# The last gathered tile of an expert mixer: second product on VectorE instead of TensorE

## The chip, the cores and the metric

One core of a Trainium2 chip runs the whole kernel in one launch. The metric is the device time of one execution in microseconds (us). The median of three executions before the change is 4364.15 us (4361.64 to 4384.96).

## What is computed

The reference is one layer of an encoder over 1280 tokens (a prompt of 256 and a sample of 1024) of width 1024, in fp32. After two mixing branches and a residual sum `x`, each token passes through a mixer of experts. It picks 16 of 16384 experts in each of 8 heads, 128 in all, and with `z` the normed token it computes

```python
u = jnp.take(u_tab, eidx, axis=0)
ve = jnp.take(v_tab, eidx, axis=0)
act = jax.nn.gelu(jnp.einsum('td,thkd->thk', zt, u).astype(jnp.float32), approximate=False) * g
return jnp.einsum('thk,thkd->td', act.astype(zt.dtype), ve)
```

`g` is a softmax over the scores of the picks. The result is added to `x`, and a last norm gives the output. The first einsum is called the u product here, the second one the second product, or v product. Both tables have 16384 rows of 1024 floats (64 MB each).

## The kernel before

The 1280 tokens are ten tiles of 128. Four tiles of the sample are *dense*: they multiply with both whole tables on TensorE (`dense`). The other six are *gathered*: for each token only the 128 picked rows of each table are fetched, by indirect DMAs that POOL issues. One such DMA fetches one row of 4 KB for each of the 128 partitions, 512 KB in all.

`experts(routes)` (L1095) walks over gathered tiles. In one turn it interleaves `u_steps` of one tile with `v_steps` of the tile before it, and a last turn runs the v product of the last tile by itself. Two of the gathered tiles belong to the prompt and go through a call of their own (L1172). The other four (`r0 + r1`, two in each list) go through the call in L1217, and `dense` is written right behind it in L1220.

- `u_steps` (L928): a slot is one of the 128 picks. Tokens lie on the partitions: POOL gathers row `ei[:, s]` of `peer_u` into a buffer `ug` (L938), and VectorE multiplies it with the normed tokens `zs` and sums along the row, in one scalar_tensor_tensor (L940).
- `v_steps` (L951): here the 128 picks of one token lie on the partitions (`eit` is the transposed index), so a gather (L969) fetches what one token needs, and TensorE sums over the partitions: the token's column of the transposed weights `actT`, put on a diagonal of a zeroed tile `zt` (L962, L963), is the stationary operand of 128 rows by 32 columns. Four gathers make a group. When the fourth is there, 16 matmuls follow (L976; two halves of 512 columns, each with four matmuls of 32 columns in four column groups of the array, and the trace has two records for each such fp32 matmul). So one tile has 32 groups and 512 records. All sums stay in one PSUM tile `acc`. At the end the residual row block is loaded by a POOL DMA (L982), added (L983), and `finish` (L992) norms the rows and stores them.
- `ring` (L925): every gathered row block, of u and of v, takes one of seven buffers of 512 KB, in the order in which the program asks for them. A buffer of v is free only when the matmuls of its group have read it.
- `dense` (L1048): one block is 128 experts; there are 128 blocks. `first(b)` loads a 512 KB block of the transposed u table, splits it into a high and a low part (L123 on ACT, L124 on VectorE), multiplies it in 24 matmuls of 512 columns (L140 to L142), applies Gelu (L1065), the weights (L1067) and another split (L159, L160). `second(g)` does this for four blocks of the v table, in 96 matmuls for each half of the columns, and adds the results into a tile in SBUF on VectorE (L1081). That is 48 matmuls a block. The loads of both tables go through the SP queue, 1 MB a block, into two raw buffers each.

The order of the instructions on each engine is fixed when the program is built (`tile.TileContext(nc, schedule_with_timeline_sim=True)`, L1293): a planner with simulated times takes, for an engine that is free, the ready instruction of the highest priority, where what is written earlier goes first. `experts` raises the steps of the v product above that:

```python
if vs:
    with tc.high_priority():
        if next(vs, "end") == "end":
            vs = None
```

At run time an engine executes its instructions in that order, and an instruction that waits holds up all that stands behind it on its engine.

Of the kernel before, what the change touches and what calls it, by code (L numbers as in the profile page):

```python
# [12 lines left out]
F32 = mybir.dt.float32  # L13
# [6 lines left out]
OP = mybir.AluOpType  # L20
# [4 lines left out]
P = 128  # L25
D = 1024
# [19 lines left out]
def ap_of(base, dims):  # L46
    return bass.AP(tensor=base.tensor, offset=base.offset, ap=[list(base.ap[0])] + [list(d) for d in dims])
# [3 lines left out]
def encoder(ctx, tc, I, O, dbg=None):  # L51
    nc = tc.nc
# [52 lines left out]
    x2d = dram.tile([T, D], F32, name="x2d")  # L105
# [67 lines left out]
    def rsqrt_small(pool, out, src, inv_n, shape, name):  # L173

        v = pool.tile(shape, F32, name=name + "v", tag=name + "v", bufs=2)
        t = pool.tile(shape, F32, name=name + "t", tag=name + "t", bufs=2)
        nc.vector.tensor_scalar(out=v, in0=src, scalar1=inv_n, scalar2=EPS, op0=OP.mult, op1=OP.add)  # L177
        nc.vector.tensor_single_scalar(out=t.bitcast(I32), in_=v.bitcast(I32), scalar=1, op=OP.logical_shift_right)  # L178
        nc.vector.tensor_scalar(out=out.bitcast(I32), in0=t.bitcast(I32), scalar1=-1.0, scalar2=float(0x5F3759DF),  # L179
                                op0=OP.mult, op1=OP.add)  # L180
        for _ in range(3):
            nc.vector.tensor_tensor(t, out, out, op=OP.mult)  # L182
            nc.vector.scalar_tensor_tensor(out=t, in0=t, scalar=-0.5, in1=v, op0=OP.mult, op1=OP.mult)  # L183
            nc.vector.scalar_tensor_tensor(out=out, in0=t, scalar=1.5, in1=out, op0=OP.add, op1=OP.mult)  # L184
# [740 lines left out]
    def ring(name):  # L925
        return pe_.tile([P, D], F32, name=name, tag="ring", bufs=RING)

    def u_steps(route):  # L928
        tt, gw, ei = route["tt"], route["gw"], route["ei"]
        zs = pe_.tile([P, D], F32, name="zs", tag="zs")  # L930
        nc.gpsimd.dma_start(zs, x2d[tt:tt + P])
        gffn = ring("gffn")
        nc.sync.dma_start(gffn, I["norm_ffn"].partition_broadcast(P))
        nc.vector.scalar_tensor_tensor(out=zs, in0=zs, scalar=route["rt"], in1=gffn, op0=OP.mult, op1=OP.mult)
        dots = pe_.tile([P, P], F32, name="dots", tag="dots", bufs=2)
        for s in range(P):
            ug = ring("ug")
            nc.gpsimd.indirect_dma_start(out=ug, out_offset=None, in_=I["peer_u"],  # L938
                                         in_offset=bass.IndirectOffsetOnAxis(ap=ei[:, s:s + 1], axis=0))
            nc.vector.scalar_tensor_tensor(out=ug, in0=ug, scalar=1.0, in1=zs, op0=OP.mult, op1=OP.mult,  # L940
                                           accum_out=dots[:, s:s + 1])
            yield
        act = pe_.tile([P, P], F32, name="act", tag="act", bufs=2)
        nc.scalar.activation(out=act, in_=dots, func=AF.Gelu)
        nc.vector.tensor_tensor(act, act, gw.rearrange("p h k -> p (h k)"), op=OP.mult)
        route["act"] = act
        yield
# [3 lines left out]
    def v_steps(route):  # L951
        tt, eit = route["tt"], route["eit"]
        acc = pps.tile([P, D], F32, name="acc", tag="acc")
        nc.tensor.transpose(acc[:, 0:P], route["act"], ident)  # L954
        actT = pe_.tile([P, 4, 32], F32, name="actT", tag="actT", bufs=2)
        nc.vector.tensor_copy(actT.rearrange("p g i -> p (g i)"), acc[:, 0:P])
        zt = zts[0]
        for b in range(8):

            h = b % 2  # L960
            o = (b + 6) % 8 * 4
            nc.vector.memset(ap_of(zt[:, h, 0, 0, o:o + 1], [[128, 4], [33, 4]]), 0.0)  # L962
            nc.vector.tensor_copy(ap_of(zt[:, h, 0, 0, b * 4:b * 4 + 1], [[128, 4], [33, 4]]), actT[:, :, b * 4:b * 4 + 4])  # L963
            for i in range(4):
                vgs = []
                for g in range(4):
                    t = g * 32 + b * 4 + i
                    vg = ring("vg")
                    nc.gpsimd.indirect_dma_start(out=vg, out_offset=None, in_=I["peer_v"],  # L969
                                                 in_offset=bass.IndirectOffsetOnAxis(ap=eit[:, t:t + 1], axis=0))  # L970
                    vgs.append(vg)
                    if g == 3:

                        for n in range(2):
                            for g_, v_ in reversed(list(enumerate(vgs))):
                                nc.tensor.matmul(acc[g_ * 32:(g_ + 1) * 32, n * 512:(n + 1) * 512], zt[:, h, g_, i],  # L976
                                                 v_[:, n * 512:(n + 1) * 512], start=b == 0 and i == 0,
                                                 stop=b == 7 and i == 3, tile_position=(0, g_ * 32), skip_group_check=True)
                    yield
        y = ring("y")  # L980
        x2r = ring("x2r")
        nc.gpsimd.dma_start(x2r, x2d[tt:tt + P])  # L982
        nc.vector.tensor_tensor(y, acc, x2r, op=OP.add)  # L983
        finish(y, x2r, tt)
        yield

    def final_gain():
        gfin = ring("gfin")
        nc.sync.dma_start(gfin, I["norm_final"].partition_broadcast(P))
        return gfin  # L990

    def finish(y, sq, tt, gfin=None):  # L992
        gfin = final_gain() if gfin is None else gfin
        ss = pe_.tile([P, 1], F32, name="fss", tag="fss")
        nc.scalar.activation(out=sq, in_=y, func=AF.Square, accum_out=ss)
        rs = pe_.tile([P, 1], F32, name="frs", tag="frs")
        rsqrt_small(pe_, rs, ss, 1.0 / D, [P, 1], "fin")
        nc.vector.scalar_tensor_tensor(out=y, in0=y, scalar=rs[:, 0:1], in1=gfin, op0=OP.mult, op1=OP.mult)  # L998
        nc.gpsimd.dma_start(O["y"][tt:tt + P], y)  # L999
# [48 lines left out]
    def dense(routes, zt, acc, dp, up, bankS, bankV):  # L1048
# [37 lines left out]
        for g in range(P // GE):  # L1086
            for b in range(g * GE + 1, (g + 1) * GE + 1):
                if b < P:
                    first(b)
            second(g)  # L1090
        gfin = final_gain()
        for t, r in enumerate(routes):
            finish(acc[:, t], ring("sq"), r["tt"], gfin)

    def experts(routes):  # L1095
        prev = None
        for r in routes + [None]:
            us = u_steps(r) if r else iter(())
            vs = v_steps(prev) if prev else iter(())
            while us or vs:  # L1100
                if us and next(us, "end") == "end":
                    us = None
# [4 lines that stand above are left out]
            prev = r  # L1107
# [13 lines left out]
    with ExitStack() as pctx:  # L1121
# [23 lines left out]
        ap = fctx.enter_context(tc.tile_pool(name="A1", bufs=1, side="left"))  # L1145
# [23 lines left out]
    for h in range(NH):  # L1169
        hgrn_out(s0, SS, h, 0, hp, 2, bankH)  # L1170
    next(prs)
    experts(rP)  # L1172
    fctx.close()
    vs_ = vsp.tile([P, 8, 512], F32, name="vs", tag="vs")
# [39 lines left out]
    up0 = ctx.enter_context(tc.tile_pool(name="DU0", bufs=1, side="right"))  # L1214
    tctx.close()
    rd, r1 = rs[:ND // P], rs[ND // P:]
    experts(r0 + r1)  # L1217
    acc = ctx.enter_context(tc.tile_pool(name="DA", bufs=1, side="left")).tile([P, ND // P, D], F32, name="acc")
    up = ctx.enter_context(tc.tile_pool(name="DU", bufs=1, side="left"))
# [78 lines left out]
```

## Time and profile before

| | before |
|---|---|
| median of 3 executions | 4364.15 us |
| the profiled execution | 4369.98 us |
| its span | 4368.2 us |
| PE busy | 3901.4 us (89%) |
| DVE busy | 2947.0 us (67%) |
| ACT busy | 1560.6 us (36%) |
| POOL busy | 1725.3 us (39%) |
| DMA | 1264.02 MB, mean 289 GB/s |

All readings below are from the profiled execution. PE is TensorE, DVE is VectorE, ACT is ScalarE, POOL is GpSimd and SP is the engine that issues most of the plain loads. The shares are means over stages that have different limits, so they say little by themselves; the slices and the tables by windows show one stage at a time. Times in them count from the start of the span. A line in a row is a line of the kernel; a helper's line stands for all of its callers.

### The profile page before, as it was taken

What the parts mean: (1) busy time and instruction counts of PE and PEld (TensorE: products, weight loads), DVE (VectorE), ACT (ScalarE), POOL (GpSimd) and SP (SyncE); (2) the same over time, 40 slices, a digit from 0 to 9 for tenths busy, and PEclk for the clock granted to TensorE, in tenths of its full rate; (3) what the DMA queues carried; (4) which work ended last, traced back from release to release, by engine and by line L of the source; (5) the groups of instructions that cost most, each with busy time, mean ns of one, the idle gap of its engine ahead of it and who ended that gap; (6) DMA issues with size and microseconds to landing.
All of it is one profiled execution on the core that took longest, in us unless ns stands there. A gap on an engine that the chain in (4) does not pass through costs nothing. (4 is left out here: it accounts for less than half of the span.)

```text
span 4368.2 us, 56612 instructions
## 1 busy us (share of the span) xinstructions
PE 3901.4 (89%) x19232; PEld 2747.1 (63%) x19232; DVE 2947.0 (67%) x7782; ACT 1560.6 (36%) x2600; POOL 1725.3 (39%) x1565
## 2 busy tenths in 40 slices
PE   7998999997687979868987399999999999999998
PEld 5787777774435733346543165777777777776676
DVE  4637987568987765876679875566666666643344
ACT  5555455453233224422101387322222222222222
POOL 0000743344444344765445312445444545434400
PEclk9999999998889999889999699999999999999999
DMA  5464999889989988999878668999999999888842
GB/s 161 124 188 136 362 342 332 314 316 319 326 288 325 330 306 286 316 345 337 311 280 283 229 234 318 331 325 339 332 335 322 344 325 346 322 317 311 309 142 67
DMA packets 508322, 1264.02 MB, mean 289 GB/s; under 512 B 49920, under 2 KB 203136, under 8 KB 505984
## 3 DMA queue, kind: packets, MB, share of 16 engines
q0 software_dynamic: 224352, 816.94, 52.0%
q1 hardware_dynamic: 197056, 354.05, 23.9%
q10 hardware_dynamic: 86624, 89.40, 5.9%
q8 instruction: 152, 2.49, 0.2%
q14 instruction: 138, 1.13, 0.1%
HBM read 1165.05 MB, written 95.16 MB: 288 GB/s over the span
## 5 line engine op out<-in xcount | busy, mean ns | idle before, releaser
L969 POOL DMA_INDIRECT vg<-peer_v,eit x768 | 823.9, 1073 | 1072.1 <-PE acc L976 429.5
L938 POOL DMA_INDIRECT ug<-peer_u,ei x768 | 887.2, 1155 | 868.7 <-DVE ug L940 407.5
L940 DVE SCALAR_TENSOR_TENSOR ug<-ug,zs 128x1024 f32<-128x1024 f32 x768 | 932.2, 1220 | 380.9 <-DMA ug<-peer_u,ei 318.7
L976 PE MATMUL acc<-vg,zt 128*32 128x512 f32 x3072 | 402.1, 644 | 126.1 <-DMA vg<-peer_v,eit 125.7
L140 PE MATMUL pm<-zth,uh 128*128 128x512 f32 x1024 | 406.7, 397 | 1.1 <-ACT gs L1039 1.1
L141 PE MATMUL pm<-ztl,uh 128*128 128x512 f32 x1024 | 405.9, 396 | 0.0
L142 PE MATMUL pm<-zth,ul 128*128 128x512 f32 x1024 | 405.7, 396 | 0.0
L140 PE MATMUL pm<-vh,ah 128*128 128x512 f32 x1024 | 399.7, 393 | 1.6 <-DVE acc L1081 1.6
L141 PE MATMUL pm<-vl,ah 128*128 128x512 f32 x1024 | 401.0, 392 | 0.0
L142 PE MATMUL pm<-vh,al 128*128 128x512 f32 x1024 | 399.3, 392 | 0.0
L123 ACT CAST vh<-vraw 128x512 fp32r<-128x512 f32 x256 | 158.3, 620 | 662.1 <-DMA vraw<-peer_v 368.0
L138 PE MATMUL pm<-xg,wraw 128*128 128x256 f32 (+1 forms) x1024 | 297.3, 443 | 4.3 <-DVE sr L855 4.3
L976 PEld LDWEIGHTS acc<-vg,zt 128*32 128x32 f32 x3072 | 83.8, 114 | 329.1 <-issue 171.8
L140 PE MATMUL pm<-hh,wh 128*128 128x512 f32 x672 | 268.7, 400 | 2.8 <-ACT gt L240 0.9
L141 PE MATMUL pm<-hl,wh 128*128 128x512 f32 x672 | 267.2, 398 | 0.0
L142 PE MATMUL pm<-hh,wl 128*128 128x512 f32 x672 | 265.3, 395 | 0.0
L1081 DVE TENSOR_TENSOR acc<-pm,acc 128x512 f32<-128x512 f32 x256 | 173.9, 688 | 126.7 <-PE pm L142 113.5
L124 DVE TENSOR_TENSOR vl<-vraw,vh 128x512 fp32r<-128x512 f32 x256 | 173.6, 689 | 119.7 <-ACT vh L123 96.2
L124 DVE TENSOR_TENSOR ul<-uraw,uh 128x1024 fp32r<-128x1024 f32 x128 | 156.6, 1223 | 140.7 <-ACT uh L123 129.6
L138 PEld LDWEIGHTS pm<-xg,wraw 128*128 128x128 f32 x1024 | 193.6, 195 | 83.0 <-issue 58.4
L140 PEld LDWEIGHTS pm<-zth,uh 128*128 128x128 f32 x1024 | 192.2, 188 | 61.4 <-issue 11.7
L140 PEld LDWEIGHTS pm<-vh,ah 128*128 128x128 f32 x1024 | 192.2, 188 | 60.0 <-issue 11.7
(361 smaller groups left out, 7263.6 us busy)
## 6 DMA issues: line engine op xcount, KB each, us to landing
uraw<-uT SPq DMA_DIRECT2D x128, 512.0 KB
vraw<-peer_v SPq DMA_DIRECT2D x256, 256.0 KB
wraw<-wi SPq DMA_DIRECT2D x84, 512.0 KB
gd<-gs ACTq DMA_DIRECT2D x16, 2048.0 KB
g<-gd ACTq DMA_DIRECT2D x32, 1024.0 KB
wraw<-wq SPq DMA_DIRECT2D x48, 512.0 KB
wraw<-wo SPq DMA_DIRECT2D x24, 512.0 KB
ug<-peer_u,ei POOLq DMA_INDIRECT x768
```

What stands on the lines that cost most here:

```text
L123: nc.scalar.copy(hi, src)
L124: (eng or nc.vector).tensor_tensor(lo, src, hi.bitcast(F32), op=OP.subtract)
L138: nc.tensor.matmul(out, w[0], x[0], start=start, stop=stop)
L140: nc.tensor.matmul(out, w[0], x[0], start=start, stop=False)
L141: nc.tensor.matmul(out, w[0], x[1], start=False, stop=False)
L142: nc.tensor.matmul(out, w[1], x[0], start=False, stop=stop)
L938: nc.gpsimd.indirect_dma_start(out=ug, out_offset=None, in_=I["peer_u"], in_offset=bass.IndirectOffsetOnAxis(ap=ei[:, s:s + 1], axis=0))
L940: nc.vector.scalar_tensor_tensor(out=ug, in0=ug, scalar=1.0, in1=zs, op0=OP.mult, op1=OP.mult, accum_out=dots[:, s:s + 1])
L969: nc.gpsimd.indirect_dma_start(out=vg, out_offset=None, in_=I["peer_v"], in_offset=bass.IndirectOffsetOnAxis(ap=eit[:, t:t + 1], axis=0))
L976: nc.tensor.matmul(acc[g_ * 32:(g_ + 1) * 32, n * 512:(n + 1) * 512], zt[:, h, g_, i], v_[:, n * 512:(n + 1) * 512], start=b == 0 and i == ...
L1081: nc.vector.tensor_tensor(acc[:, t, ns], pm, acc[:, t, ns], op=OP.add)
```

## The change

A new generator `v_slots` does the second product with tokens on the partitions, as the u product does: it loads the residual rows into an SBUF tile `vacc`, gathers the picked rows of `peer_v` slot by slot with the index `ei`, and adds each, times the token's weight, with one scalar_tensor_tensor on VectorE. It needs neither transposed weights nor PSUM. A route that has an `acc` takes it; only the last tile of `r1` gets one, and its pool takes 4 KB per partition of SBUF up to the end. The other five gathered tiles keep `v_steps`. The weights `act`, the ring of seven buffers and the priority of the v steps are as before.

```diff
+    def v_slots(route):
+
+        tt, ei, act = route["tt"], route["ei"], route["act"]
+        acc = route["acc"].tile([P, D], F32, name="vacc", tag="vacc", bufs=1)
+        nc.gpsimd.dma_start(acc, x2d[tt:tt + P])
+        for s in range(P):
+            vg = ring("vg")
+            nc.gpsimd.indirect_dma_start(out=vg, out_offset=None, in_=I["peer_v"],
+                                         in_offset=bass.IndirectOffsetOnAxis(ap=ei[:, s:s + 1], axis=0))
+            nc.vector.scalar_tensor_tensor(out=acc, in0=vg, scalar=act[:, s:s + 1], in1=acc, op0=OP.mult, op1=OP.add)
+            if s % 2:
+                yield
+        finish(acc, ring("sq"), tt)
+        yield
+
...
-            vs = v_steps(prev) if prev else iter(())
+            vs = (v_slots if "acc" in prev else v_steps)(prev) if prev else iter(())
...
+    vp = ctx.enter_context(tc.tile_pool(name="VA", bufs=1, side="right"))
+    for r in r1[1:]:
+        r["acc"] = vp
     experts(r0 + r1)
```

## Rows read from the trace of the kernel before

**Rows 1.** The page: the span, and PE, DVE, granted clock, DMA in 40 slices.
```profile
span 4368.2 us, 56612 instructions
...
PE   7998999997687979868987399999999999999998
...
DVE  4637987568987765876679875566666666643344
...
PEclk9999999998889999889999699999999999999999
DMA  5464999889989988999878668999999999888842
```
**Rows 2.** Windows of 100 us: length, PE, PEld, DVE, ACT, POOL busy, clock, DMA, GB/s.
```profile
3900.00:4000.00 100.00, 100.00 (x504) 67.92 (x505) 38.70 (x55) 26.12 (x38) 41.43 (x42) 1.00 0.89 312
4000.00:4100.00 100.00, 97.62 (x494) 65.85 (x493) 35.62 (x53) 24.22 (x36) 44.34 (x43) 1.00 0.88 310
...
4200.00:4300.00 100.00, 100.00 (x436) 81.48 (x435) 46.41 (x63) 29.44 (x43) 0.00 (x0) 1.00 0.36 110
```
**Rows 3.** Timeline of POOL around the start of the last tile's gathers: start, duration.
```profile
3826.91 0.94 POOL L969 DMA_INDIRECT vg<-peer_v,eit  x1 [0.30 <-issue]
3827.85 0.58 POOL L982 DMA_DIRECT2D x2r<-x2d  x1
3840.88 0.95 POOL L969 DMA_INDIRECT vg<-peer_v,eit  x1 [12.45 <-PE acc L976]
```
**Rows 4.** Waits from 3829 to 4160 us: total, times, longest.
```profile
POOL vg L969 <- PE acc L976: 151.4, 31, 12.4
...
PE acc L976 <- DMA vg<-peer_v,eit: 3.4, 3, 2.4
```
**Rows 5.** Timeline of PE: one group of the last tile between two dense matmuls.
```profile
4063.28 0.39 PE L142 MATMUL pm<-vh,al 128*128 128x512 f32 x1
...
4063.60 1.92 PE L976 MATMUL acc<-vg,zt 128*32 128x512 f32 x16
...
4065.45 0.50 PE L140 MATMUL pm<-vh,ah 128*128 128x512 f32 x1
```
**Rows 6.** The chain that ended last: the same step in two successive rounds of four blocks.
```profile
4279.52 0.47 PE pm L142 x2
4323.77 0.47 PE pm L142 x2
```
**Rows 7.** Groups on DVE from 4180 to 4312.75 us, twelve dense blocks alone.
```profile
L1081 DVE TENSOR_TENSOR acc<-pm,acc 128x512 f32<-128x512 f32 x24 | 16.6, 690 | 17.5 <-PE pm L142 17.4
L124 DVE TENSOR_TENSOR vl<-vraw,vh 128x512 fp32r<-128x512 f32 x24 | 16.5, 691 | 21.5 <-ACT vh L123 21.4
L124 DVE TENSOR_TENSOR ul<-uraw,uh 128x1024 fp32r<-128x1024 f32 x12 | 14.7, 1225 | 25.8 <-ACT uh L123 25.8
L160 DVE TENSOR_TENSOR al<-ge,ah 128x512 fp32r<-128x512 f32 x12 | 8.3, 691 | 6.2 <-ACT ah L159 6.2
L1067 DVE TENSOR_TENSOR ge<-ge,g 128x512 f32<-128x512 f32 x12 | 8.2, 685 | 0.0
```
**Rows 8.** Groups on DVE from 3829 to 4176 us.
```profile
L998 DVE SCALAR_TENSOR_TENSOR y<-y,frs,gfin 128x1024 f32<-128x1024 f32 x2 | 2.6, 1285 | 0.1
...
L983 DVE TENSOR_TENSOR y<-acc,x2r 128x1024 f32<-128x1024 f32 x2 | 2.4, 1214 | 2.3 <-PE acc L976 2.3
L963 DVE COPY zt<-actT 128x16 f32<-128x16 f32 x8 | 1.2, 168 | 10.4 <-issue 7.8 <-PE acc L976 2.6
```
**Rows 9.** Timeline where u gathers run alone, DVE and POOL.
```profile
1846.72 0.93 POOL L938 DMA_INDIRECT ug<-peer_u,ei  x1 [0.30 <-issue]
...
1850.34 1.22 DVE L940 SCALAR_TENSOR_TENSOR ug<-ug,zs 128x1024 f32<-128x1024 f32 x1
...
1851.49 1.22 DVE L940 SCALAR_TENSOR_TENSOR ug<-ug,zs 128x1024 f32<-128x1024 f32 x1
1851.53 1.99 POOL L938 DMA_INDIRECT ug<-peer_u,ei  x1 [0.30 <-issue]
```
**Rows 10.** Windows, columns as in rows 2, where u gathers run alone.
```profile
1800.00:1900.00 100.00, 76.32 (x355) 35.27 (x354) 94.26 (x183) 41.84 (x101) 78.05 (x63) 0.86 0.95 342
```
**Rows 11.** Windows of 50 us, columns as in rows 2: the highest DMA rate.
```profile
500.00:550.00 50.00, 47.24 (x212) 38.24 (x211) 49.56 (x114) 18.79 (x25) 34.78 (x26) 1.00 0.98 364
```
**Rows 12.** Waits from 1700 to 1900 us.
```profile
ACT pn L606 <- DVE mn L602: 54.5, 18, 6.6
PEld pm L138 <- ACT pn L606: 44.3, 17, 5.3
```
**Rows 13.** Windows: u and v gathers beside dense; all engines, then L938 alone on POOL.
```profile
3200.00:3300.00 100.00, 100.00 (x470) 74.61 (x469) 69.75 (x116) 28.85 (x44) 49.29 (x43) 1.00 0.93 332
...
3200.00:3300.00 100.00, 23.17 (x20) 1.00 0.93 332
```
**Rows 14.** The page: the costliest groups, the matmuls of the gathered v product.
```profile
L976 PE MATMUL acc<-vg,zt 128*32 128x512 f32 x3072 | 402.1, 644 | 126.1 <-DMA vg<-peer_v,eit 125.7
```

## The prediction

> **What bounds the kernel now.** I read the slices first, because the change touches one stage only. From slice 23 on, about 2500 us, PE shows nines to the end while DVE falls to 6 and then to 3 and 4 [rows 1]: the dense stage is bound by TensorE, and VectorE has room on average. Next the windows of 100 us. Around 4000 us PE is busy 98 to 100 us in 100, DVE 36 to 39, at full clock and with DMA at 0.88 [rows 2]. Third, POOL's timeline and the list of waits say what paces the gathers of the last tile. Its first one is issued at 3840.88, when a group of the tile before it frees its buffers [rows 3], and POOL waited 151 us in that stage for L976, while PE waited 3.4 us for gathers [rows 4]. So the ring sets the pace: a group of four must be complete and read before the next can be. POOL does nothing but that there: 42 or 43 gathers in 100 us, one in 2.35 us [rows 2].
>
> **What the change takes away.** One group lies between two dense matmuls that start 2.17 us apart [rows 5]. Four dense blocks, 192 matmuls, take 44.25 us [rows 6], so one takes 0.230 us and a block 11.06 us. The group costs 2.17 - 0.23 = 1.94 us, and the 32 groups of a tile **62 us** of an engine that has no other slack. The transpose and copy of the weights, 16 small writes of `zt` and the sum L983 go too, some 0.17 to 1.2 us each on DVE [rows 8]; with them under 5 us of DVE, counted at nothing since they wait for no one's path.
>
> **What it adds.** 128 scalar_tensor_tensors of 128x1024 on DVE. L940 has this form, with two fp32 operands in SBUF and a sum written out besides: back to back they start 1.15 us apart [rows 9]. L998, without that sum, shows 1.285 us [rows 8], pipeline ends included. I take 1.15 us, 147 us in all; with 1.285 it would be 164.
>
> The Trainium skill (Vector Engine (DVE) Microarchitecture Reference, Points that are easy to get wrong) says that this instruction with two non-bf16 sources in SBUF runs at half throughput; doubling the step measured back to back would make it 2.3 us, an estimate, and with the formulas below the sum +185 us instead of +61, 4549 us. The trace disagrees, with 1.15 us for that very form, and the measurement decides: that way gets no chance below.
>
> **What it moves.** The residual load, now the first DMA on POOL rather than the last, stands where L982 of the tile before is followed by 12.45 us of waiting [rows 3]: nothing, and without that cover 0.6 us. As many gathers as before are issued, but their buffers come free one by one, as with u. The end of the tile (norm and store) stays hidden behind dense work, which goes on for some 190 us after it now [rows 1, 2]. The 4 KB of SBUF show no price in the trace; I take none, since no tile of the stage is made smaller.
>
> **The wait it adds.** Each new DVE instruction waits for a gather, and behind it in DVE's fixed order stand the dense stage's splits, weights and sums. TensorE waits for those. One dense block needs (16.6 + 16.5 + 14.7 + 8.3 + 8.2) / 12 = 5.36 us of DVE [rows 7]. So the question is how much dense work the order puts between two slots. Call it w, in us of DVE. In the stage of the 128 slots DVE then does 128w / 5.36 = 23.9w blocks, which are 264w us of PE.
>
> The stage's length: if DVE sets it, 128 x (1.15 + w). If the DMA does, the bytes are 128 x 0.524 = 67.1 MB of gathers and 23.9w x 1.05 = 25.1w MB of tables. The nearest rows give 342 GB/s at 0.95 of the DMA's time [rows 10] and 364 at 0.98 [rows 11]; with the middle, 353, it is 190 + 71w us, which is the longer one up to w = 0.75. POOL gives about the same floor: where u gathers run alone, 63 are issued in 100 us [rows 10], 1.59 us each, and POOL is then busy 78 us with them and loses 0.3 us between two, 97 in all. An issue takes 0.93 us, and up to 1.99 while such DVE instructions run [rows 9].
>
> What PE can't do in that stage has to be done after it. The net change is the stage, minus 264w, minus the 62 us: **128 - 193w** while the DMA rules, 85 - 136w beyond.
>
> For w the trace of before has two ends. Where u gathers run alone, DVE is busy 94.26 us in 100, of which 63 x 1.15 = 72.5 are slots; that leaves 21.8 / 63 = 0.35 us [rows 10]. Where u and v gathers run together beside dense work, 20 u slots stand in 69.75 us of DVE, which leaves 2.3 us [rows 13]. The new stage is like the first: one kind of gather, with buffers freed one by one. In the second the groups of v held most of the ring. And the new slots have the raised priority, which u's have not, so the order takes a slot whenever it believes one to be ready, and dense work only in the gaps. The stage of u gathers alone also shows what follows [rows 10, 12]: PE at 76 us in 100, with 54.5 us of ACT waiting for a small DVE result and 44.3 us of PE's weight loads waiting for that ACT. With w = 0.35 the stage is 215 us, in which PE does 92 us of dense work; it loses 123 and gets 62 back. The sum is **+61 us**. On the profiled execution, 4370 us, that is 4431; it lies 5.8 us above the median of the runs, from which I forecast 4364 + 61 = **4425 us**. If w goes to 0, which [rows 10] can't exclude, it is +128 us.
>
> PE's clock in such a stage: with PE at 76 us in 100 the mean granted was 0.86, between the levels of 1.2 and 2.4 GHz [rows 10]. It costs nothing as long as DVE or the DMA, not PE, ends the wait, and full clock is there where PE is full [rows 2].
>
> **The rivals.** (1) *VectorE carries both; faster.* If the order leaves w = 1.08 or more, that is, if it expects a gather no oftener than every 2.23 us, PE never runs dry and the whole 62 us are gained: 4302 us. For it: the pace of 2.35 us and DVE at 36 to 39 us in 100 [rows 2], and the 2.3 us between slots beside dense work [rows 13]. Against: that pace was made by groups in the ring, which go, and where u gathers run alone one comes every 1.59 us [rows 10]. The point from which it is faster at all is w = 0.66. Chance 0.33, with a part of it between 4302 and 4342.
> (2) *It balances.* Around w = 0.66 the lost and gained time of PE cancel, 4342 to 4386 us. Nothing in the rows picks this value. Chance 0.09.
> (3) *Slots back to back.* If the order believes that gathers arrive as fast as POOL issues them undisturbed, 0.93 + 0.3 = 1.23 us [rows 9], w is 0.08 and the dense stage all but stops for 196 us: +113, 4477 us. There are pairs like that in the trace [rows 9], but no long run of them in the mean of 100 us [rows 10]. It is the upper part of my forecast, 0.15 of its 0.58.
> (4) *Not as stated.* If more or fewer than one tile took the new way, the count of L976 would not fall from 3072 [rows 14] to 2560. `r1` has two tiles and `r1[1:]` one, so I give this nothing.
>
> **How the numbers follow.** A measurement of this kernel can tell about 0.5% from no change, 22 us. Slower by more is the forecast, with (3): 0.58. Within it is (2): 0.09. Faster is (1): 0.33. Cases of both signs hold most of the chance, so the range takes in both: from 4298, the full gain with the few us of PE's waits for gathers, to 4480, w = 0.06. The slower case by itself is 4390 to 4480.
>
> **What the changed profile would show.** L976 x2560. A stretch after about 3840 us with 128 gathers in 200 to 230 us, DMA at 0.95 or more, DVE above 85 us in 100 with waits for `vg`, PE clearly below 80 us, and PE's loads or ACT waiting for DVE. After it dense work alone, 11.06 us a block, and an end that is later by the stage's lost time. I am wrong if PE stays full beside the slots: then w was over 1, and the gathers came no oftener than before. I am wrong in size if DVE idles for gathers that come slower than 1.7 us, or if an added slot takes clearly other than 1.15 us.

## The result and the profile after

The change is **faster**, by 1.4 to 1.9%: 4307.53 us median of four executions (4296.1 to 4308.96), against 4371.23 of the kernel before in the same runs. The measured ratio is 0.9833 with a 95% interval of 0.981 to 0.9856; the two medians alone give 0.985. I had forecast 4425 us and slower; 4302 us was the rival in which VectorE carries both. The profiled execution took 4296.1 us, with a span of 4294.2.

The slices of the changed kernel, PE and DVE:

```profile
span 4294.2 us, 55849 instructions
...
PE   6998999997777988878988389999999999999998
...
DVE  4637988567988774986679985566666666679974
```

PE has the same nines to the end as before [rows 1]. DVE now has 7 and 9 in the slices where it had 3 and 4. The windows of 100 us around 4000, columns as in rows 2:

```profile
3900.00:4000.00 100.00, 100.00 (x434) 81.19 (x433) 93.90 (x104) 30.26 (x47) 53.60 (x42) 1.00 0.96 338
4000.00:4100.00 100.00, 100.00 (x433) 80.98 (x432) 92.88 (x102) 27.36 (x42) 56.03 (x42) 1.00 0.95 336
```

DVE went from 36 to 39 us up to 93, DMA from 0.88 to 0.96 of the time, and PE is still full, at full clock. All its 433 or 434 matmuls are dense ones; before, 160 of some 500 records were the groups of the tile. And POOL issues 42 gathers in 100 us, **the same as before** [rows 2]. The same tile's gathers and slots, and the waits between 3826 and 4130 us (engine, line, what it waited for: total, times, longest):

```profile
L994 POOL DMA_INDIRECT vg<-peer_v,ei x128: 932/1144/3482, 3826.1 to 4118.0; - x128
L996 DVE SCALAR_TENSOR_TENSOR vacc<-vg,act,vacc x128: 1271/1278/1287, 3830.6 to 4129.6; 128x1024 f32<-128x1024 f32 x128
...
POOL vg L994 <- DVE vacc L996: 100.2, 73, 4.2
...
DVE vacc L996 <- DMA vg<-peer_v,ei: 1.9, 1, 1.9
```

The last two lines say who is late. DVE waited 1.9 us for a gather in the whole stage, POOL 100 us for DVE to free a buffer. So at run time the gathers are early, and it is DVE's fixed order that sets their pace. The 128 slots take 3830.6 to 4130.9, 300 us: 2.35 us each. A slot followed by other work takes DVE 1.20 us (the timeline below), so w, what lies between two slots, is 2.35 - 1.20 = **1.15 us**, not 0.35. DVE's idle time, 6 to 7 us in 100, is in this number. The prediction took its 0.35 from the busy time; counted like that, the two windows of 100 us give 93.4 / 42.6 - 1.15 = 1.04.

The pace is about what dense work leaves. Alone it keeps DVE busy 46 us in 100 while PE is full [rows 2]. The other 54 would hold 45 slots of 1.20 us, one in 2.2 us, as an estimate. So DVE is nearly full of both kinds of work, and none of it makes PE wait: the list of PE's waits from 3800 us on has a single one, of 0.3 us.

The time before the last tile varies by some 10 us from execution to execution: its first gather starts at 3826.1 us here and at 3816.8 in a later profile of the same kernel. So I measure the stage from that gather to the end of the span. Before it was 4368.2 - 3840.9 = 527 us [rows 1, 3], after it is 4294.2 - 3826.1 = **468 us**, 59 us less. But the two don't start at the same dense work: 1907 dense matmuls (L140 to L142; 48 a block, and the 96 of `second` are those of both halves of the columns together) lie in the stage before and 1950 in the stage after, and at 0.230 us the 43 are 10 us. For the same dense work the stage is **69 us** shorter. The groups were worth 62, and PE's waits for their gathers 3.4 [rows 4]. L976 fell to x2560.

### The profile page after: what moved, and what is told of

Read it like the earlier page. It is cut to its first block, busy times and chain, and to the rows that moved or that the text cites. A ratio compares the mean times of both kernels' runs of the same rounds, so it can differ in the third digit from the quotient of the medians.

```text
span 4294.2 us, 55849 instructions
## 1 busy us (share of the span) xinstructions
PE 3842.8 (89%) x18719; PEld 2742.8 (64%) x18719; DVE 3091.5 (72%) x7892; ACT 1558.0 (36%) x2600; POOL 1747.9 (41%) x1565
## 3 DMA queue, kind: packets, MB, share of 16 engines
q14 instruction: 140, 1.15, 0.1%
## 4 chain that ended last, share of the span: by engine, by line
PE 45%; DMA 8%; issue 7%; DVE 5%; POOL 2%; ACT 1%; POOLq 0%; SPq 0%; DVEq 0%; ACTq 0%
PE pm L140 10%; PE pm L142 10%; PE pm L141 10%; PE acc L976 5%; DMA vg<-peer_v,eit 4%; PE pm L138 3%; PE pm L1053 3%; DMA ug<-peer_u,ei 2%; DVE ug L940 2%; PE pm L1034 1%; POOL ug L938 1%; PE pm L624 1%; PE pm L618 1%; DMA g<-gd 1%; ACT gs L1054 1%
## 5 line engine op out<-in xcount | busy, mean ns | idle before, releaser
L938 POOL DMA_INDIRECT ug<-peer_u,ei x768 | 879.3, 1145 | 849.2 <-DVE ug L940 357.0
L969 POOL DMA_INDIRECT vg<-peer_v,eit x640 | 685.7, 1071 | 896.8 <-DVE ug L940 431.2
L976 PE MATMUL acc<-vg,zt 128*32 128x512 f32 x2560 | 344.6, 660 | 123.4 <-DMA vg<-peer_v,eit 122.6
L140 PE MATMUL pm<-zth,uh 128*128 128x512 f32 x1024 | 405.5, 396 | 2.8 <-ACT uh L123 1.7
L142 PE MATMUL pm<-zth,ul 128*128 128x512 f32 x1024 | 405.9, 396 | 0.0
L142 PE MATMUL pm<-vh,al 128*128 128x512 f32 x1024 | 396.1, 392 | 0.0
L140 PE MATMUL pm<-vh,ah 128*128 128x512 f32 x1024 | 393.0, 392 | 0.3 <-DVE acc L1096 0.3
L140 PE MATMUL pm<-hh,wh 128*128 128x512 f32 x672 | 270.0, 402 | 4.3 <-ACT gt L240 2.4
L142 PE MATMUL pm<-hh,wl 128*128 128x512 f32 x672 | 266.4, 396 | 0.0
L123 ACT CAST uh<-uraw 128x1024 fp32r<-128x1024 f32 x128 | 134.3, 1050 | 351.6 <-PE pm L141 318.0
L976 PEld LDWEIGHTS acc<-vg,zt 128*32 128x32 f32 x2560 | 70.8, 116 | 295.7 <-issue 147.3
L142 PEld LDWEIGHTS pm<-zth,ul 128*128 128x128 f32 x1024 | 192.5, 188 | 57.8 <-issue 11.7
L140 PEld LDWEIGHTS pm<-zth,uh 128*128 128x128 f32 x1024 | 192.5, 188 | 56.8 <-issue 6.7
L141 PEld LDWEIGHTS pm<-ztl,uh 128*128 128x128 f32 x1024 | 192.4, 188 | 53.9 <-issue 8.4
```

The costliest lines, as they stand in the source:

```text
L123: nc.scalar.copy(hi, src)
L140: nc.tensor.matmul(out, w[0], x[0], start=start, stop=False)
L141: nc.tensor.matmul(out, w[0], x[1], start=False, stop=False)
L142: nc.tensor.matmul(out, w[1], x[0], start=False, stop=stop)
```

## The experiments

### What spaces the slots

Two waits can hold a slot back in the order: for its gather, and, through `vacc`, for the slot before it. The second I had not thought of: the u slots write to columns of their own and are independent. Four kernels take away one wait, the other or both, or make the gather smaller; each leaves out part of the last tile's product, as its expectation says.

**Chain kept, gathers out.**

```diff
-            vg = ring("vg")
-            nc.gpsimd.indirect_dma_start(out=vg, ...
+            if s == 0:
+                vg = ring("vg")
+                nc.gpsimd.indirect_dma_start(out=vg, ...
```

> Leaves out 127 of the 128 gathers of the last tile: every slot adds the same row block again, so no slot waits for a gather; the chain through the sum stays. Theory A (two waits space the slots, the gather and the sum that the slot before has to finish; either alone makes the order put dense work between two slots): PE stays full, the time is that of the changed kernel, 4305 us within 15. Theory B (the gathers alone space them, as the prediction had it): the slots stand back to back for 128 x 1.2 = 154 us, dense work stops, 4305 + 150 = 4455 us.

**Gathers kept, chain out.**

```diff
-            nc.vector.scalar_tensor_tensor(out=acc, in0=vg, scalar=act[:, s:s + 1], in1=acc, op0=OP.mult, op1=OP.add)
+            nc.vector.scalar_tensor_tensor(out=vg, in0=vg, scalar=act[:, s:s + 1], in1=acc, op0=OP.mult, op1=OP.add)
```

> Leaves out the sum: each slot writes its product into its own buffer, so no slot waits for the slot before; the gathers stay. Theory A: the gathers still space the slots, 4305 to 4330 us, a little more dense work lost than in the changed kernel. Theory C (the chain alone spaces them): w falls to the 0.35 us of the prediction and the time is 4425 us.

**Neither.** Only the first seven slots gather; each slot writes `vg` from `vacc`.

```diff
-            nc.gpsimd.indirect_dma_start(out=vg, ...
-            nc.vector.scalar_tensor_tensor(out=acc, in0=vg, ...
+            if s < 7:
+                nc.gpsimd.indirect_dma_start(out=vg, ...
+            nc.vector.scalar_tensor_tensor(out=vg, in0=acc, ...
```

> Leaves out 121 gathers and the sum: 128 slots on VectorE that wait neither for a gather nor for each other. Theory A: now they crowd VectorE, in runs, and PE runs dry: 60 to 150 us above the changed kernel, 4365 to 4455 us. Theory D (dense work has VectorE first whatever the slots wait for): as the changed kernel, 4305 us.

**Half rows, chain out.** The table is read as 32768 rows of 512 columns, and a slot writes over the buffer that its gather filled.

```diff
-            nc.gpsimd.indirect_dma_start(out=vg, out_offset=None, in_=I["peer_v"],
+            nc.gpsimd.indirect_dma_start(out=vg[:, :512], out_offset=None, in_=I["peer_v"].rearrange("e (n j) -> (e n) j", n=2),
...
-            nc.vector.scalar_tensor_tensor(out=acc, in0=vg, ...
+            nc.vector.scalar_tensor_tensor(out=vg, in0=acc, ...
```

> No sum, as in the run without the chain, and gathers of half a row: each slot writes a product of the residual rows over its buffer, so it waits for the gather but not for another slot. It tells whether the bytes of the gathers are what held w up there. Theory E (they are): w lies between that run's and that of the run with neither wait, near 0.65 us, PE runs dry for 30 to 60 us in the stage, 4335 to 4360 us. Theory F (any gather does it, whatever its size): PE loses no more than in the run without the chain, 4315 to 4330 us.

Measured, with the stage from first gather to end and w from the first to the last slot of each trace, as above. The kernels ran on different chips, so the ratios, each to the kernel before in the same runs, say more than the times. Every stage but that of the kernel before holds 1950 dense matmuls.

| kernel | time, us | ratio to before (95%) | stage, us | w, us |
|---|---|---|---|---|
| before | | | 527 | |
| changed | 4307.5 | 0.981 to 0.986 | 468 | 1.15 |
| chain alone | 4292.5 | 0.975 to 0.989 | 466 | 1.21 |
| gathers alone | 4328.7 | 0.987 to 0.993 | 486 | 0.97 |
| half gathers alone | 4341.5 | 0.991 to 0.995 | 508 | 0.65 |
| neither | 4359.0 | 0.995 to 0.999 | 523 | 0.52 |

The slots' rows behind the column w: after the colon the shortest, median and longest slot in ns, then the first and the last start, in the order of the table's last four lines, one fence for each kernel.

```profile
L997 DVE SCALAR_TENSOR_TENSOR vacc<-vg,act,vacc x128: 1273/1280/1289, 3843.0 to 4149.8; 128x1024 f32<-128x1024 f32 x128
```
```profile
L996 DVE SCALAR_TENSOR_TENSOR vg<-vg,act,vacc x128: 1270/1281/1324, 3848.4 to 4124.5; 128x1024 f32<-128x1024 f32 x128
```
```profile
L996 DVE SCALAR_TENSOR_TENSOR vg<-vacc,act x128: 1265/1273/1333, 3825.4 to 4060.5; 128x1024 f32<-128x1024 f32 x128
```
```profile
L997 DVE SCALAR_TENSOR_TENSOR vg<-vacc,act x128: 1275/1326/1393, 3838.7 to 4057.8; 128x1024 f32<-128x1024 f32 x128
```

The chain alone keeps PE full with one gather instead of 128 (theory B falls). The gathers alone do it nearly: the stage is 18 us longer than that of the changed kernel (theory C falls). With half the bytes it is 40 us longer, with neither wait 55 (theory D falls, and the time stays a little under the range of theory A). So theory A holds: either wait makes the order put dense work between the slots. Theory E holds in its numbers: with half the bytes a gather spaces the slots less. That kernel differs from the run without the chain in one more thing, the slot's first operand, `vacc` for `vg`, and no run has that alone. The windows of 100 us show the crowding that I had forecast, in the kernel with neither wait, and below them are two of PE's waits from 3800 to 4330 us (total, times, longest):

```profile
3900.00:4000.00 100.00, 76.60 (x307) 59.91 (x305) 100.00 (x104) 21.04 (x30) 0.00 (x0) 0.93 0.27 79
4000.00:4100.00 100.00, 85.29 (x342) 68.48 (x343) 86.75 (x113) 28.56 (x45) 0.56 (x1) 0.91 0.38 120
...
PE pm L140 <- DVE acc L1097: 27.5, 6, 7.7
PE pm L142 <- DVE al L160: 10.3, 3, 4.9
```

DVE is full while the slots last, up to 4059 us, PE idles 23 and 15 us in 100, and the waits name the dense sums and splits, which stand behind slots. The stall costs PE more than its idle time: 307 and 342 matmuls where a full window has 434 are 219 fewer, 50 us at 0.230, against 38 us idle. The rest goes with the granted clock, on average 0.93 and 0.91 there, between the levels of 1.2 and 2.4 GHz. DVE's timeline of the same kernel (start, duration, line) and then of the chained one without gathers shows how the orders differ:

```profile
3949.37 1.33 DVE L997 SCALAR_TENSOR_TENSOR vg<-vacc,act 128x1024 f32<-128x1024 f32 x1
3950.57 1.33 DVE L1083 TENSOR_TENSOR ge<-ge,g 128x512 f32<-128x512 f32 x2
3951.77 7.31 DVE L997 SCALAR_TENSOR_TENSOR vg<-vacc,act 128x1024 f32<-128x1024 f32 x6
3958.95 0.73 DVE L124 TENSOR_TENSOR vl<-vraw,vh 128x512 fp32r<-128x512 f32 x1
```
```profile
4000.19 1.22 DVE L124 TENSOR_TENSOR ul<-uraw,uh 128x1024 fp32r<-128x1024 f32 x1
4001.32 0.69 DVE L1083 TENSOR_TENSOR ge<-ge,g 128x512 f32<-128x512 f32 x1
4001.93 1.28 DVE L997 SCALAR_TENSOR_TENSOR vacc<-vg,act,vacc 128x1024 f32<-128x1024 f32 x1
4003.12 0.69 DVE L160 TENSOR_TENSOR al<-ge,ah 128x512 fp32r<-128x512 f32 x1
4003.72 2.61 DVE L997 SCALAR_TENSOR_TENSOR vacc<-vg,act,vacc 128x1024 f32<-128x1024 f32 x2
```

Independent slots come up to six in a row and hold DVE for 7.3 us; chained ones mostly come with a dense instruction between them. Counted in the DVE timelines, the 128 slots stand in 63 runs with neither wait, in 83 with gathers alone, in 95 in the changed kernel (two of them of six) and in 102 with the chain alone (none longer than three). A slot with such work behind it takes 4003.12 - 4001.93 = 1.19 us.

### Does the priority matter?

The raised priority of the last tile's v steps was part of my argument for crowding.

```diff
-                    with tc.high_priority():
+                    with tc.high_priority() if r else ExitStack():
```

> The changed kernel without the raised priority for the last tile's v steps. Theory A: what spaces the slots are their waits, and dense work is written later anyway, so nothing moves: 4305 us within 15. If the raised priority mattered, as the prediction used it, slots would now give way: later gathers, PE full, and the time at most that of the changed kernel, with the 128 slots spread over more than 304 us.

It took 4301.37 us (ratio 0.980 to 0.988), and its slots stand as before, 300 us for 128:

```profile
L996 DVE SCALAR_TENSOR_TENSOR vacc<-vg,act,vacc x128: 1269/1280/1291, 3840.7 to 4139.8; 128x1024 f32<-128x1024 f32 x128
```

The priority decides nothing here: the stage is 468 us again. As theory A has it, in the last turn of `experts` only dense work is left to compete, and it is written later anyway.

### What the slots cost, and how far it goes

**Slots of 64 columns.** `acc`, `vg` and `in1` are cut to `[:, :64]`.

> The changed kernel with slots of 64 columns (the other 960 of the last tile's product are left out): the gathers and the removal from TensorE without the work on VectorE. Theory A (the slots cost PE nothing): 4305 us within 12. If the slots cost something: lower by that.

4297.52 us (0.982 to 0.988), beside 4286.67 for the changed kernel in the same runs. Nothing is gained by taking the work away from VectorE. The run is not a clean removal, though: its stage is 482.5 us, 14 longer than with whole slots, and PE is busy only 91 us in 100 between 4000 and 4100, so the order changed too. That the 147 to 164 us lie wholly beside PE, as the rival had it, rests on the changed kernel itself, where PE is full and waits 0.3 us.

**Every slot twice.**

```diff
             nc.vector.scalar_tensor_tensor(out=acc, in0=vg, scalar=act[:, s:s + 1], in1=acc, op0=OP.mult, op1=OP.add)
+            nc.vector.scalar_tensor_tensor(out=acc, in0=vg, scalar=act[:, s:s + 1], in1=acc, op0=OP.mult, op1=OP.add)
```

> The changed kernel with every slot's instruction twice (the sum counts each row twice). Theory A: VectorE now needs 128 x 2.4 = 307 us for the slots and the full dense need of 5.36 us a block no longer fits beside them, so PE runs dry for the first time: by the prediction's own formula in its region where VectorE sets the stage, w near 1.4 us gives 128 x (2.4 + 1.4) - 264 x 1.4 = 117 us lost by PE, of which what lies behind the last block is hidden: 4350 to 4420 us. Theory D (dense work always has VectorE first): PE stays full and the slots only end later, at most 30 us above the changed kernel, 4335 us.

4381.59 us (ratio 1.003 to 1.006). The number lies in the range of theory A, but for another reason. Windows, and the second instruction of each slot:

```profile
4100.00:4200.00 100.00, 100.00 (x434) 81.30 (x434) 94.00 (x104) 29.42 (x44) 27.93 (x21) 1.00 0.71 224
4200.00:4300.00 100.00, 53.49 (x232) 43.10 (x230) 96.41 (x94) 9.48 (x15) 47.84 (x31) 0.79 0.57 172
...
L997 DVE SCALAR_TENSOR_TENSOR vacc<-vg,act,vacc x128: 1272/1280/1286, 3809.5 to 4343.0; 128x1024 f32<-128x1024 f32 x128
```

PE stays full until dense work ends, near 4253 us, and the slots trail to 4344. So here chained slots don't take DVE from dense work even when there are too many of them: they are what waits, and the sum of the tile becomes the end. D was right that PE stays full, and wrong by 47 us on the time.

**More tiles.** The loop that hands out `vp` takes in the first tile of `r1`, then also the second of `r0`, then the first.

```diff
-    for r in r1[1:]:
+    for r in r1:
```

> Both tiles of the second list go to VectorE. Theory A: another 32 groups leave PE beside dense work, VectorE goes from 65 to about 90 us in 100 there, DMA stays near 0.95: another 45 to 62 us, 4245 to 4260 us. Theory B: with u and v slots together VectorE is over its limit and dense work waits: no gain or a loss, 4300 us or more.

> The second tile of the first list goes to VectorE too, so every second product that runs beside dense work. Theory A: PE alone would give 4305 - 124 = 4181 us, but the 494 MB that move from 2700 us to the end in the changed kernel need 1430 us at 345 GB/s, so the DMA ends it near 4150 us and its tail comes on top: 4180 to 4220 us. Theory B: VectorE over its limit: no better than with two tiles.

> All four tiles of the sample go to VectorE. The first one's second product runs from about 1950 to 2650 us, where VectorE is busy 67 to 94 us in 100 and PE 30 to 92. Theory A: there the groups cost PE little and the slots cost VectorE 154 us: 20 to 120 us slower than with three tiles. Theory B (PE is what counts everywhere): faster than three tiles by up to 60 us.

Two tiles took 4270.83 us, three 4310.13 and four 4340.9. The ratios to the kernel before are 0.9789 (0.975 to 0.983), 0.9864 (0.984 to 0.989) and 0.9944 (0.992 to 0.997). For three tiles theory B came out, and the 4180 to 4220 us of theory A were some 90 us too low; four are 31 us slower than three, as theory A had it. Two tiles looked 37 us better than one (4270.83 against 4307.53), but in runs made apart. So both ran again, side by side, with a kernel of two tiles and half rows:

> The changed kernel once more, beside the version with two tiles on the same chip: 4305 us within 10.

> The version with two tiles once more. Theory A (each tile frees PE until VectorE and the DMA are full, which happens on the way through the second tile): 4270 us within 10, below the changed kernel by 25 to 45 us. Theory B (one tile is all that VectorE carries): no difference from the changed kernel.

> Two tiles, but their v gathers fetch half a row for each slot and both halves of the sum use it, so the last two tiles move 67 MB less while VectorE does the same. It tells what took the 26 us that the second tile fell short of 62. Theory DMA (0.97 to 1.00 busy there): PE is full again and the time 4240 to 4250 us. Theory VectorE (96 us in 100): 4265 to 4275 us as with whole rows.

One tile 4286.67 us (ratio 0.979 to 0.984), two 4281.62 (0.978 to 0.983): **no difference** that these runs can tell. One tile was 18 us under the 4305 expected, but its ratio agrees with the first one, 0.9833. My 4270 and its 25 to 45 us were too good, and theory B's outcome is what stands. Two tiles with half rows: 4245.26 (0.970 to 0.976). Windows of 200 us beside dense work, for two tiles and then for two with half rows; the slots of the fifth gathered tile, the first of the two on VectorE, run up to 3650 and 3715 us, the last u slots up to 3781 and 3859:

```profile
3400.00:3600.00 200.00, 181.85 (x751) 141.97 (x749) 189.12 (x235) 50.56 (x75) 123.13 (x96) 0.97 0.97 353
3600.00:3800.00 200.00, 183.74 (x754) 145.63 (x755) 191.52 (x295) 54.43 (x83) 129.58 (x99) 0.96 0.99 369
```
```profile
3400.00:3600.00 200.00, 192.95 (x827) 154.02 (x825) 180.35 (x229) 56.84 (x86) 107.02 (x82) 1.00 0.79 261
3600.00:3800.00 200.00, 192.91 (x821) 154.91 (x822) 180.70 (x266) 54.75 (x84) 108.75 (x86) 0.98 0.84 293
```

With two tiles DVE is at 95 us in 100 and the DMA at 0.97 to 0.99, and PE runs dry. A full PE does 868 dense matmuls in 200 us; here it does 751 and 754, which is 117 + 114 fewer, at 0.230 us 53 us of PE, and 43 fewer in the next window make it 63. That is all of the 62 that the second tile frees. With half rows the DMA falls to 0.8, 143 of the 231 missing matmuls are back, and so are 36 us. So most of the second tile's gain goes with the bytes of the gathers. Whether the full DMA takes it at run time isn't shown. The order differs too, as half rows alone brought w from 0.97 to 0.65 above, and DVE falls here from 95 to 90 us in 100. With two tiles the largest of PE's waits (2640 to 4300 us) is for a split on DVE, not for a load:

```profile
PE pm L141 <- DVE vl L124: 24.2, 17, 4.3
```

Three tiles are no better than one, and four are worse. The changed kernel, with one tile, is as good as any of these versions that compute the whole.

The kernel with three tiles shows one thing more: from 3600 to 3700 us its last u slots run beside dense work without any v slot. They are independent, with whole rows, without the raised priority.

```profile
3600.00:3700.00 100.00, 91.28 (x377) 71.37 (x375) 93.67 (x154) 25.11 (x37) 63.75 (x49) 0.97 0.98 363
```

50 slots start in this window, so w is 93.67 / 50 - 1.15 = 0.72 us, counted as the prediction counted its 0.35. PE runs dry beside them, at 91 us in 100.

## Why the prediction was wrong

- **What PE gets back: right.** 62 us forecast for the 32 groups; for the same dense work the stage is 69 us shorter, of which 3.4 are waits for gathers.
- **A slot's price: right within 5% where other work follows.** 1.15 us from the u slots, 1.19 to 1.20 measured between a slot and other work; between two chained slots 1.32, 15% more. That VectorE would take 2.3 us for two fp32 sources shows in none of these runs.
- **The formula: right in its trend, off by 10 to 15 us.** Before the 62 us are taken off, what PE loses in the stage is 128 x (1.15 + w) - 264w = 147 - 136w where DVE rules. With w as a slot's whole time less 1.15 us, that is 8 us for gathers alone (w = 1.02), 52 for half gathers (0.70) and 70 for neither (0.57). Against the changed kernel the stages lost 18, 40 and 55. So break-even lies below 0.57 and not at 0.66, which came from the formula's half where the DMA rules; none of these three runs was in that half. One term is too large: 5.36 us a block adds up durations that overlap at their ends (0.69 us long, 0.60 apart in the timelines above). DVE busy 46.41 us in 100 [rows 2] is 5.13 a block.
- **The step that failed: "The new stage is like the first: one kind of gather, with buffers freed one by one", hence w = 0.35.** The stage gave 1.15, or 1.04 in the prediction's own count, and its sign for being wrong came true: PE stays full beside the slots. A share read beside attention [rows 10] was carried to a stage beside dense work. Two things differ. First, what stands between the slots: the same kind of u slots beside dense work leaves 0.72, and the new slots without their chain 0.97. That alone turns the sign of the forecast, for the kernel without the chain is still faster than the one before (0.987 to 0.993). Why attention leaves so little is open: that there was simply less to put between the slots is an argument, and the 54.5 us that ACT waited there for DVE [rows 12] show that some work was wanted. Second, the chain: the u slots are independent, the new ones are not, and the diff says so, with `acc` as an input and as the output. Chained alone, without gathers, they leave 1.21. A wait of some kind is needed for all this: with neither w is 0.52, and most of the gain is gone.
- **The raised priority: no effect**, by the run without it.
- **The rival that came true** rested on the right rows: 2.35 us a gather beside dense work [rows 2]. The changed kernel has 2.35 us a slot. I had set it aside because "that pace was made by groups in the ring, which go". The groups went, and the pace of the DVE order took their place. That the two paces are equal is chance, since one was made by groups in the ring and the other by DVE full of slots and dense work. So the rival was right in its outcome, and in VectorE having the room, but not in why a slot comes every 2.35 us.
- **The sign of the added wait.** I looked for what stands behind a slot that waits for a gather. In the trace DVE waits for gathers 1.9 us. What starved PE, in the kernel with neither wait, was dense work behind slots that came in runs; chained slots come in shorter and fewer runs.

## What to carry to other kernels

A share of other work read between the instructions of one stage can't be carried to another stage unless both the neighbours and the waits are the same. Here the same kind of slot left 0.35 us beside attention and 0.72 beside dense work. The operands in the diff say whether the waits are the same. Where an accumulation moved to another engine as a chain of dependent instructions, the planned order of this kernel filled the gaps between them with other work, and the engine was less crowded than by as many independent instructions. An engine with room on average takes such work for nothing until something else is full: the first tile gave its 62 us, and the second met a DVE busy 95 us in 100 and a DMA at 0.97 to 0.99 at once.

## What the runs showed of the hardware

Two dependent scalar_tensor_tensors of 128x1024 start 1.32 us apart, two independent ones 1.20. From DVE's timeline, six in a row in the changed kernel take 7.88 us, six in a row in the kernel with neither wait 7.31 (above); without the last one's 1.28 or 1.33 us that is five steps of 1.32 or 1.20. The kernel with gathers alone reads the same two operands as the changed one and shows 1.20 as well.

```profile
4063.80 7.88 DVE L996 SCALAR_TENSOR_TENSOR vacc<-vg,act,vacc 128x1024 f32<-128x1024 f32 x6
```

POOL's time for a gather grew beside these instructions: 168.6 us for 128 between 3826 and 4130, 1.32 us each and up to 3.48, against the 0.94 of an undisturbed one [rows 3]. With slots of 64 columns it was 129.8 us for 128, 1.01 each, so it is the whole slots that lengthen it.

```profile
3826.00:4130.00 304.00, 168.61 (x128) 1.00 0.95 339
```

The Trainium skill (GPSIMD Engine Reference, Specifications) names SBUF interfaces that GpSimd shares with VectorE, contended by VectorE instructions with two SBUF inputs; the slots are such, and the trace agrees with the direction. POOL is not what limits here: it waits 100 us for buffers.
